# Longer TensorE matmul durations in the planner of an encoder block

## The chip, the cores and the metric

The kernel runs on one core of a Trainium2 chip. The metric is the device time of one execution in microseconds (us). Five engines run side by side, each with its own instruction stream taken in order: PE (TensorE, matmuls), DVE (VectorE), ACT (ScalarE), POOL (GpSimd) and SP (SyncE, which here issues DMAs).

## The reference

One layer of a hybrid encoder, 256 tokens with 16 meta tokens put in front (272 positions), width 2048, all in fp32:

```python
h = concat([meta, x])                               # 272 x 2048
hn = rmsnorm(h, mix_norm_g)
q_a, k_a, v_a, cq, ckv, k_pe = split(hn @ w_in)     # 3 x 1024, 512, 256, 64 columns
oa = neighbourhood_attention(q_a, k_a, v_a, ...)    # 8 heads of 128, window on a 4 x 64 grid
ob = mla_attention(cq, ckv, k_pe, ...)              # 8 heads; low-rank q and kv, rotary key
h = h + concat([rmsnorm(oa), rmsnorm(ob)]) @ w_out
hn = rmsnorm(h, ffn_norm_g)
g, u = hn @ w_gate, hn @ w_up                       # 2048 -> 5632
h = h + (silu(depthwise_conv3(g)) * u) @ w_down     # 5632 -> 2048
return h[:, 16:]                                    # meta tokens dropped
```

## The kernel before

**Arithmetic.** Every fp32 number is kept as two parts of a shorter fp32 format that PE takes faster (`F32R`): a high part, copied by ACT (`whi<-raw`, L251), and a low part, a subtract on DVE (`wlo<-raw,whi`, L255). A product of two such numbers is three matmuls: high by high, high by low, low by high. `mm3` (L734 to L736) issues these three for one 128 x 128 block of weights and 256 to 272 columns of tokens; `mm2` (L2056, L2057), in the MLP, puts the high and low part of the tokens beside each other in one matmul of 512 columns, with a second of 256. Other products go through `MM`, a list of matmuls whose lines are L291. Some of the MLP's weights go through a seven-product scheme (Strassen's, in Winograd's form), for which DVE adds and subtracts quarters of weight blocks (`more_raw`, `sums`) and of results (`mt`).

**Stages.** The program goes through the input projection with the two attentions woven into it (to about 300 us of the span), the output projection (to about 400 us), gate and up of the MLP (to about 850 us) and the down projection. Weights are read once, in pieces of 128 x 1024, in an order that is written out: `raw` (5 buffers) is filled by a DMA, split into `whi` and `wlo` (4 buffers each), and used by PE. The attention helpers are small chains between the large matmuls. The ones that the text speaks of:

- Sums over the head's dimension of squares (`late<-scr,late` on DVE, then the matmul pair `bank<-late,ones_r` on PE, in `keys`).
- Sums for the few meta queries (`small_sums`): a cast on DVE (`sq8r<-sq`, L267), a subtract on POOL (`sq8r<-sq,sq8r`, L279), then two-column matmuls (`bank<-ones_r,sq8r`, L291).
- The rotary embedding (`rope`): a DMA swaps the halves of a tile (`scr<-scr`), DVE multiplies with the tables (`scr<-scr,consts`), then follow `mqr`, the parts of the rotated queries. There are four pairs of heads on each side, so each chain comes four times or eight.

**What sets the order.** The kernel orders its instructions itself, when the program is built. Each piece of work is a Python generator, a thread, that yields requests: an engine with a duration in ns, a free buffer, or an event. `Flow.run` holds one clock for each engine and takes, again and again, the thread whose next step could start first: the larger of the engine's clock and the thread's own time with a latency (700 ns where PE follows another engine), then by priority, then by age. It sets the clock to start plus duration, and the thread then emits its instruction. So the order on each engine's stream follows from these clocks. The durations are formulas: 93 + 0.833 n for an ACT operation of n elements, 68 + 1.04 n on DVE, 90 + 2.7 n on POOL (3.9 n after 400 us), a DMA's bytes over 350 with 2000 ns more (3200 after 400 us). On the chip each engine takes its stream in order and waits by semaphores for what it needs, so a duration in the planner changes no instruction, only the order.

Of the kernel before, what the change touches and what calls it, by code (L numbers as in the profile page):

```python
# [17 lines left out]
SEQ = 256  # L18
# [200 lines left out]
def encoder_block(ctx: ExitStack, tc: tile.TileContext, io):  # L219
# [15 lines left out]
    def size(ap):  # L235
        n = 1
        for s in ap.shape[1:]:
            n *= s
        return n
# [37 lines left out]
    def PTT(out, a, b, op):  # L277
        yield "pool", 90 + (2.7 if fl.cur.t < 4e5 else 3.9) * size(out)
        nc.gpsimd.tensor_tensor(out, a, b, op)  # L279

    def cost(l, r):
        n, m = size(r), l.shape[-1]
        if r.dtype != F32R:
            return max(1.69 * n, 3.33 * m, 50)
        return 0.445 * n + 3 if n >= 256 else max(0.84 * n, 0.84 * m, 27)

    def MM(items):

        yield "pe", sum(cost(l, r) for _, l, r, _, _ in items)
        for o, l, r, start, stop in items:  # L290
            nc.tensor.matmul(o, l, r, start=start, stop=stop)  # L291
# [86 lines left out]
    class RowPair:  # L378
# [50 lines left out]
        def used(self, kind):  # L429
            self.left[kind] -= 1  # L430
            if self.left[kind] == 0:
                by_sums = kind in ("more", "sums") or kind == "two" and self.mode == "third"
                fl.put(made if by_sums else raws, self.at[kind])
# [102 lines left out]
    n = len(others) - BEHIND  # L536
# [174 lines left out]
    def block():  # L711

        p, o = pieces[at[0]], at[1]
        if o % p.step == 0:
            yield p.ready[o // p.step]
        return p.hi[:, o : o + P], p.lo[:, o : o + P]
# [13 lines left out]

    def mm3(ps, xhi, xlo, start, stop):
        whi, wlo = yield from block()
        yield "pe", 3 * (0.445 * size(xhi) + 3)
        nc.tensor.matmul(ps, whi, xhi, start=start, stop=False)  # L734
        nc.tensor.matmul(ps, whi, xlo, start=False, stop=False)  # L735
        nc.tensor.matmul(ps, wlo, xhi, start=False, stop=stop)  # L736
        used()
# [37 lines left out]
    for g in range(0, FC // 2 if MID_SUMS else 0, MID_SUMS or 1):  # L775
        n = min(MID_SUMS, FC // 2 - g)
# [971 lines left out]
    def project(tiles, n, slots=acc):  # L1748

        pss = []  # L1750
        for _ in range(tiles):
            pss.append((yield from one(slots)))
        for k in range(KC):
            if at[0] < 2:
                yield from first_products(pss, k, n)
                continue
            yield ev_xs[k]
            for ps in pss:
                yield from mm3(ps[:, :n], hl[k][:, 0, :n], hl[k][:, 1, :n], k == 0, k == KC - 1)
        return pss  # L1760
# [37 lines left out]
    def attention_weights():  # L1798
# [8 lines left out]
        def up_queries(m):  # L1807
            pss = []
            for c in range(3):
                ps = yield from one(acc)  # L1810
                for k in range(4):
                    yield ev_cq[k]
                    yield from mm3(ps[:, :NT], cq[k][0], cq[k][1], k == 0, k == 3)
                pss.append(ps)
            fl.spawn(mla_queries(m, pss))

        def up_keys(m):
            yield ev_ckv
            for c in range(2):
                ps = yield from one(acc)  # L1820
                for k in range(2):
                    yield from mm3(ps[:, :L], ckv[k][0], ckv[k][1], k == 0, k == 1)
                fl.spawn(mla_keys(m, c, ps))
# [228 lines left out]
    def mm2(ps, x, n, start, stop):  # L2052

        whi, wlo = yield from block()
        yield "pe", 347
        nc.tensor.matmul(ps, whi, x, start=start, stop=False)  # L2056
        nc.tensor.matmul(ps[:, :n], wlo, x[:, 0, :], start=False, stop=stop)  # L2057
        used()

    def mm_up(ps, k):  # L2060
        yield from mm2(ps, hl[k][:, :, :SEQ], SEQ, k == 0, k == KC - 1)

    def mlp_weights():
        pss, f = [], 0
        for p, kind, which, q in work:
            if kind in ("gate", "up"):
                if q == 0:
                    pss = []
                    for _ in range(2):
                        pss.append((yield from one(acc)))  # L2070
                for k in range(4 * q, 4 * q + 4):
                    for c in range(2):
                        yield from (mm_gate if kind == "gate" else mm_up)(pss[c], k)
                if q == 3:
                    for c in range(2):
                        fl.spawn((gated if kind == "gate" else tile_up)(2 * which + c, pss[c]))
                if kind == "up" and which == FC // 2 - 1:
                    hl_free(q)
            elif kind == "scheme":
                yield from scheme_products(p, which)  # L2080
            else:
                if f == 0:
                    ps = yield from one(acc)
                for _ in range(p.n // P):
                    yield ev_act[f]
                    if which < KC - ST - 1:
                        yield from mm2(ps, act[:, f], SEQ, f == 0, f == FC - 1)
                    else:
                        yield from mm3(
                            ps[:, :SEQ], act[:, f, 0, :], act[:, f, 1, :], f == 0, f == FC - 1  # L2090
                        )
                    f += 1
                if f == FC:
                    fl.spawn(down_out(which, ps))
                    f = 0
# [376 lines left out]
```

## Time and profile before

| | |
|---|---|
| time, median of 3 runs | 1103.25 us (1103.39, 1103.25, 1102.38) |
| span of the profiled execution | 1102.0 us; no time of its own is given beside it, the runs lie 0.4 to 1.4 us over it |
| granted clock of PE | 0.999 |
| busy: PE, DVE, ACT, POOL | 99%, 92%, 68%, 11% |
| instructions on PE, DVE, ACT, POOL | 8164, 1935, 1507, 199 |
| DMA, mean over the span | 238 GB/s |

The span is from the profiled execution's first instruction to its last. "Busy" is the share of the span in which an engine had an instruction under way. Matmuls overlap in PE's pipeline, so a row's duration (some 280 ns for 256 columns) is longer than the time from one start to the next; what a matmul costs in a full queue is that second time.

### The profile page before, as it was taken

The page shows a single profiled execution, that of the slowest core. Times are in us where ns is not written, and L with a number is a line of the kernel's source. Part 1 is how long each engine was busy: PE and PEld are TensorE (multiplying, and loading weights), DVE is VectorE, ACT ScalarE, POOL GpSimd, SP SyncE. Part 2 cuts the span into 40 slices and gives each one's busy share as a digit, 9 for nine tenths or more (in the row PEclk, how much of TensorE's full clock was granted, in tenths as well). Part 3 has the DMA queues.
Part 4 walks back from the last instruction along what each step waited for, and adds up shares of the span by engine and source line. Part 5 has one row for each costly group of instructions (what it writes and reads, how often), then busy time and mean ns, then how long its engine had stood idle before and what let it go on. Part 6 is the DMA issues. An engine that isn't in the chain of part 4 may idle for free.

```text
span 1102.0 us, 22408 instructions
## 1 busy us (share of the span) xinstructions
PE 1094.0 (99%) x8164; PEld 1046.5 (95%) x8164; DVE 1015.0 (92%) x1935; ACT 751.1 (68%) x1507; POOL 120.8 (11%) x199
## 2 busy tenths in 40 slices
PE   9999999999999999999999999999999999999998
PEld 9999999999999999999999999999999999888887
DVE  8969887988878989999999999999999989999997
ACT  8688978888646776656666666665666656566663
POOL 3211222232443400000000000000000000000001
PEclk9999999999999999999999999999999999999999
DMA  9765678567877778655666656758788878699891
GB/s 327 253 230 176 197 218 236 149 203 182 255 207 208 229 256 324 215 193 192 224 221 209 225 192 237 262 193 285 264 299 287 292 237 322 205 320 336 302 331 45
DMA packets 82166, 262.72 MB, mean 238 GB/s; under 512 B 9224, under 2 KB 13320, under 8 KB 82056
## 3 DMA queue, kind: packets, MB, share of 16 engines
q1 hardware_dynamic: 78600, 252.38, 66.0%
q0 software_dynamic: 3168, 8.65, 5.2%
q8 instruction: 64, 1.05, 0.4%
q14 instruction: 46, 0.38, 0.1%
q10 hardware_dynamic: 288, 0.27, 0.1%
HBM read 243.82 MB, written 34.08 MB: 252 GB/s over the span
## 4 chain that ended last, share of the span: by engine, by line
PE 87%; ACT 5%; DVE 4%; DMA 2%; issue 1%; SPq 0%; POOL 0%; DVEq 0%; ACTq 0%; POOLq 0%
PE bank L291 27%; PE bank L734 14%; PE bank L735 14%; PE bank L736 14%; PE bank L2056 11%; PE bank L2057 6%; PE bank L297 2%; ACT whi L251 1%; DVE wlo L255 1%; DVE scr L263 1%; ACT scr L251 1%; DMA scr<-scr 1%; ACT qraw L251 0%; DMA early<-in_w_down_s 0%; DMA raw<-in_w_cq 0%
## 5 line engine op out<-in xcount | busy, mean ns | idle before, releaser
L251 ACT ACTIVATE whi<-raw 128x512 fp32r<-128x512 f32 (+2 forms) x493 | 354.1, 738 | 158.5 <-PE bank L735 54.6
L255 DVE TENSOR_TENSOR wlo<-raw,whi 128x512 fp32r<-128x512 f32 (+2 forms) x493 | 408.0, 848 | 30.7 <-ACT whi L251 29.8
L734 PE MATMUL bank<-hl,whi 128*128 128x258 f32 (+1 forms) x1208 | 347.8, 288 | 0.1
L735 PE MATMUL bank<-hl,whi 128*128 128x258 f32 (+1 forms) x1208 | 343.7, 285 | 0.0
L736 PE MATMUL bank<-hl,wlo 128*128 128x258 f32 (+1 forms) x1208 | 343.1, 284 | 0.2 <-DVE wlo L255 0.2
L736 PEld LDWEIGHTS bank<-hl,wlo 128*128 128x128 f32 x1208 | 229.7, 190 | 0.6 <-DVE wlo L255 0.4
L735 PEld LDWEIGHTS bank<-hl,whi 128*128 128x128 f32 x1208 | 229.3, 190 | 0.1
L734 PEld LDWEIGHTS bank<-hl,whi 128*128 128x128 f32 x1208 | 228.2, 189 | 0.8 <-ACT scr L251 0.3
L291 PE MATMUL bank<-whi,act 128*128 128x256 f32 (+1 forms) x574 | 143.5, 302 | 0.0
L2056 PE MATMUL bank<-hl,whi 128*128 128x512 f32 x384 | 136.6, 395 | 0.0
L2057 PE MATMUL bank<-hl,wlo 128*128 128x256 f32 x384 | 107.7, 280 | 0.0
L291 PEld LDWEIGHTS bank<-whi,act 128*128 128x128 f32 x574 | 100.2, 189 | 5.2
L251 ACT ACTIVATE whi<-more_raw 128x1024 fp32r<-128x1024 f32 x69 | 71.8, 1040 | 42.7 <-DVE more_raw L255 22.7
L291 PE MATMUL bank<-wlo,act 128*128 128x256 f32 (+1 forms) x287 | 86.8, 302 | 0.0
L2056 PEld LDWEIGHTS bank<-hl,whi 128*128 128x128 f32 x384 | 72.1, 188 | 14.9
L255 DVE TENSOR_TENSOR wlo<-more_raw,whi 128x1024 fp32r<-128x1024 f32 x69 | 82.6, 1196 | 3.2 <-ACT whi L251 3.1
L279 POOL TENSOR_TENSOR halves<-halves,resT 128x256 f32<-128x256 f32 x4 | 3.0, 784 | 703.9 <-ACT halves L251 703.9
L2057 PEld LDWEIGHTS bank<-hl,wlo 128*128 128x128 f32 x384 | 72.4, 188 | 0.0
L291 PE MATMUL bank<-whi,sin 128*128 128x256 f32 (+1 forms) x248 | 69.0, 325 | 0.0
L251 ACT ACTIVATE whi<-halves 128x1024 fp32r<-128x1024 f32 (+2 forms) x57 | 52.2, 936 | 22.4 <-PE bank L291 7.5
L255 DVE TENSOR_TENSOR wlo<-halves,whi 128x1024 fp32r<-128x1024 f32 (+2 forms) x57 | 60.4, 1074 | 0.5 <-ACT whi L251 0.3
L291 PEld LDWEIGHTS bank<-wlo,act 128*128 128x128 f32 x287 | 54.3, 189 | 2.2
(323 smaller groups left out, 2216.1 us busy)
## 6 DMA issues: line engine op xcount, KB each, us to landing
raw<-in_w_gate SPq DMA_DIRECT2D x88, 512.0 KB, 5.1
raw<-in_w_in SPq DMA_DIRECT2D x52, 512.0 KB, 4.5
raw<-in_w_up SPq DMA_DIRECT2D x48, 512.0 KB, 4.5
raw<-in_w_up_s SPq DMA_DIRECT2D x40, 512.0 KB, 4.4
raw<-in_w_out SPq DMA_DIRECT2D x32, 512.0 KB, 5.1
sin<-s_down SPq DMA_DIRECT2D x28, 512.0 KB, 6.5
raw<-in_w_down_m SPq DMA_DIRECT2D x21, 512.0 KB, 5.4
s_down<-sums SPq DMA_DIRECT2D x20, 512.0 KB, 6.5
```

The lines of the kernel that those rows point to most:

```text
L251: nc.scalar.activation(out, in_, f, **kw)
L255: nc.vector.tensor_tensor(out, a, b, op)
L263: nc.vector.scalar_tensor_tensor(out, a, s, b, op0, op1)
L279: nc.gpsimd.tensor_tensor(out, a, b, op)
L291: nc.tensor.matmul(o, l, r, start=start, stop=stop)
L297: nc.tensor.transpose(o, i, ident[:n, :n])
L734: nc.tensor.matmul(ps, whi, xhi, start=start, stop=False)
L735: nc.tensor.matmul(ps, whi, xlo, start=False, stop=False)
L736: nc.tensor.matmul(ps, wlo, xhi, start=False, stop=stop)
L2056: nc.tensor.matmul(ps, whi, x, start=start, stop=False)
L2057: nc.tensor.matmul(ps[:, :n], wlo, x[:, 0, :], start=False, stop=stop)
```

## The change

The planner's duration of a large matmul is another formula; all else in the program text is the same.

```diff
+    def stream(n):
+        return n / 2.4 + 0.436 * -(-n // 16) + 4.7
+
     def cost(l, r):
         n, m = size(r), l.shape[-1]
         if r.dtype != F32R:
             return max(1.69 * n, 3.33 * m, 50)
-        return 0.445 * n + 3 if n >= 256 else max(0.84 * n, 0.84 * m, 27)
+        return stream(n) if n >= 256 else max(0.84 * n, 0.84 * m, 27)
...
     def mm3(ps, xhi, xlo, start, stop):
         whi, wlo = yield from block()
-        yield "pe", 3 * (0.445 * size(xhi) + 3)
+        yield "pe", 3 * stream(size(xhi))
...
     def mm2(ps, x, n, start, stop):
         whi, wlo = yield from block()
-        yield "pe", 347
+        yield "pe", stream(2 * SEQ) + stream(SEQ)
```

The formulas give, in ns: 118.3 for 116.9 at 256 columns, 119.6 for 117.8 at 258, 125.4 for 124.0 at 272, 232.0 for 230.8 at 512; a step of `mm2` 350.4 for 347.

The program has the same instructions on each engine. PE's are the same to the operand, except for the buffer in which a split weight or a helper's tile lies. On PE the first difference in order stands at row 254 (about 36 us), the last at row 3234 (about 400 us): between them the large matmuls keep their order, and the helpers' matmuls stand 3 to 40 matmuls earlier or later among them. On DVE some 1020 rows stand elsewhere, on ACT 700, on SP 236, on POOL 77, and these run to the end of the program. The new function moves the line numbers of all that follows by three.

In the order below a row is one instruction, or several alike (x2): line, operation, output and inputs (the number after a name is that of the tile or buffer), and the size. DVE, around 180 us, before; `late_164<-scr_176` is the last operand of the sum of squares for which PE waits at 185.55 us:

```order
L255 TENSOR_TENSOR wlo_92<-raw_84,whi_88 128x512
L267 CAST sq8r_212<-sq_210 128x8
L255 TENSOR_TENSOR scr_182<-scr_182,consts 128x258
L255 TENSOR_TENSOR wlo_89<-raw_80,whi_85 128x512
L263 SCALAR_TENSOR_TENSOR scr_177<-scr_183,scr_177 128x272
L263 SCALAR_TENSOR_TENSOR v_235<-cols_222,emc_c 128x4
L255 TENSOR_TENSOR wlo_89<-raw_80,whi_85 128x512
L263 SCALAR_TENSOR_TENSOR v_235<-bank_76,emc_s 4x1
L263 SCALAR_TENSOR_TENSOR scr_184<-scr_177,scr_184 128x272
L255 TENSOR_TENSOR mqr_265<-scr_178,mqr_265 64x258
L263 SCALAR_TENSOR_TENSOR scr_181<-scr_181,gains,scr_184 128x272
L255 TENSOR_TENSOR late_164<-scr_176,late_164 128x272
```

and with the change:

```order
L263 SCALAR_TENSOR_TENSOR scr_179<-scr_184,scr_179 128x272
L255 TENSOR_TENSOR wlo_92<-raw_84,whi_88 128x512
L263 SCALAR_TENSOR_TENSOR scr_182<-scr_179,scr_182 128x272
L255 TENSOR_TENSOR scr_177<-scr_177,consts 128x258
L267 CAST sq8r_212<-sq_210 128x8
L263 SCALAR_TENSOR_TENSOR scr_180<-scr_180,gains,scr_182 128x272
L255 TENSOR_TENSOR wlo_92<-raw_84,whi_88 128x512
L255 TENSOR_TENSOR wlo_89<-raw_80,whi_85 128x512
L255 TENSOR_TENSOR late_163<-scr_180,late_163 128x272
L255 TENSOR_TENSOR late_164<-scr_176,late_164 128x272
```

The rope product (`consts`) has gone from row 361 to row 355 of DVE and stands ahead of the `sq8r` cast instead of behind it; `late_164` has gone from row 370 to 361. The cast's own place has gone from row 360 to 356.

PE around 194.8 us, before, where the sums of the meta queries (`ones_r,sq8r_213`) follow an early block of weights:

```order
L735 MATMUL bank_72<-hl_100,whi_85 128x272
L736 MATMUL bank_72<-hl_100,wlo_89 128x272
L291 MATMUL bank_76<-ones_r,sq8r_213 4x2 x2
L734 MATMUL bank_75<-hl_100,whi_85 128x272
L735 MATMUL bank_75<-hl_100,whi_85 128x272
```

and with the change:

```order
L294 MATMUL bank_76<-mkp_268,qs_209 36x272
L737 MATMUL bank_75<-hl_101,whi_86 128x272
L738 MATMUL bank_75<-hl_101,whi_86 128x272
L739 MATMUL bank_75<-hl_101,wlo_90 128x272
L294 MATMUL bank_77<-ones_r,sq8r_213 4x2 x2
L737 MATMUL bank_72<-hl_101,whi_86 128x272
```

The sums now stand behind the next block of weights (`hl_101`) and behind the products with the small queries (`qs`), 37 matmuls later; the cast that feeds them stands at row 394 of DVE where it stood at 393.

DVE at 738 to 744 us, in the seven-product scheme, before:

```order
L255 TENSOR_TENSOR mt_5445<-mt_5445 128x128 x2
L255 TENSOR_TENSOR wlo_89<-more_raw_5449,whi_85 128x1024
L255 TENSOR_TENSOR sums_93<-mt_5445,sums_93 128x256
L255 TENSOR_TENSOR more_raw_5449<-raw_80 128x512
L255 TENSOR_TENSOR more_raw_5449<-raw_80,more_raw_5449 128x256
L255 TENSOR_TENSOR more_raw_5449<-more_raw_5449,raw_80 128x256
L255 TENSOR_TENSOR wlo_90<-raw_81,whi_86 128x1024
L255 TENSOR_TENSOR wlo_91<-raw_80,whi_87 128x512
L255 TENSOR_TENSOR wlo_91<-raw_80,whi_87 128x256
L255 TENSOR_TENSOR sums_93<-mt_5445,sums_93 128x256
```

and with the change:

```order
L255 TENSOR_TENSOR sums_93<-mt_5467,sums_93 128x256
L255 TENSOR_TENSOR wlo_89<-more_raw_5472,whi_85 128x1024
L255 TENSOR_TENSOR sums_93<-mt_5468,sums_93 128x256
L255 TENSOR_TENSOR more_raw_5472<-raw_84 128x512
L255 TENSOR_TENSOR more_raw_5472<-raw_84,more_raw_5472 128x256
L255 TENSOR_TENSOR more_raw_5472<-more_raw_5472,raw_84 128x256
L255 TENSOR_TENSOR wlo_90<-raw_81,whi_86 128x1024
L255 TENSOR_TENSOR wlo_91<-raw_84,whi_87 128x512
```

The second of the two `sums`, which stood behind the `wlo` pieces, now stands ahead of them, and the two `mt` have gone further up.

## The prediction

> **What bounds the kernel now.** I read the page first: the busy shares and the chain that ended last.
>
> ```profile
> span 1102.0 us, 22408 instructions
> PE 1094.0 (99%) x8164; PEld 1046.5 (95%) x8164; DVE 1015.0 (92%) x1935; ACT 751.1 (68%) x1507; POOL 120.8 (11%) x199
> PE 87%; ACT 5%; DVE 4%; DMA 2%; issue 1%; SPq 0%; POOL 0%; DVEq 0%; ACTq 0%; POOLq 0%
> ```
>
> TensorE (PE) is busy 99% of the span and carries 87% of the chain. A change that only reorders instructions, with the same matmuls, can therefore gain only what PE idles now, and can lose whatever new waits it puts in front of PE. So the next view is the table of busy time by window, where PE's idle time is the length of a window less its busy time.
>
> ```profile
> 0.00:50.00 50.00, 48.45 (x369) 47.47 (x370) 42.63 (x88) 38.87 (x88) 16.06 (x38) 1.00 0.86 305
> 50.00:100.00 50.00, 49.47 (x397) 48.14 (x396) 41.54 (x105) 40.87 (x122) 7.17 (x16) 1.00 0.59 196
> 100.00:150.00 50.00, 49.75 (x417) 49.02 (x416) 43.94 (x125) 44.90 (x150) 11.91 (x27) 1.00 0.67 203
> 150.00:200.00 50.00, 48.45 (x402) 47.87 (x401) 42.17 (x114) 41.18 (x131) 14.94 (x27) 1.00 0.76 220
> 250.00:300.00 50.00, 49.83 (x414) 49.32 (x413) 44.39 (x118) 38.65 (x116) 18.38 (x28) 1.00 0.78 216
> 300.00:400.00 100.00, 100.00 (x816) 99.14 (x815) 84.62 (x151) 63.45 (x125) 35.15 (x35) 1.00 0.76 224
> 600.00:700.00 100.00, 100.00 (x780) 97.17 (x779) 98.44 (x181) 63.49 (x102) 0.00 (x0) 1.00 0.64 224
> sum 1102.00, PE 1093.97 PEld 1046.54 DVE 1015.04 ACT 751.14 POOL 120.81; mean PE 78.14 PEld 74.75 DVE 72.50 ACT 53.65 POOL 8.63
> ```
>
> (Columns: window, its length, then busy us and count of PE, PEld, DVE, ACT, POOL, then the granted clock, DMA share, GB/s.) PE idles 1.55 us in the first 50 us, 0.53, 0.25 and 1.55 in the next three windows, 0.17 in 250:300, none in 300:400 and none in the MLP. That is 4.05 us; the sum row's 8.03 us holds besides it the last 4 us, when the output leaves. The list of waits names the causes:
>
> ```profile
> PE bank L291 <- POOL sq8r L279: 1.1, 3, 0.7
> PE bank L866 <- DVE em L863: 1.1, 1, 1.1
> PE bank L291 <- DVE late L255: 0.9, 1, 0.9
> PE bank L291 <- ACT whi L251: 0.3, 1, 0.3
> PE bank L736 <- DVE wlo L255: 0.2, 1, 0.2
> PE bank L291 <- ACT p L251: 0.2, 1, 0.2
> ```
>
> The `em` wait of 1.1 us is the start of the program; it stays. What reordering can take is 4.05 - 1.1 = 2.95 us, in the attention stage. One number decides what the new durations mean, the start-to-start time of matmuls in a full queue, from the chain of waits (start, length, what):
>
> ```profile
> 450.66 1.42 PE bank L291 x12
> 950.16 8.32 PE bank L291 x36
> ```
>
> 12 matmuls of 256 columns take 1.42 us, 118 ns each; 36 of 512 take 8.32 us, 231 ns each.
>
> **The change part by part.** Formula in `cost`: `stream(256)` is 256/2.4 + 0.436*16 + 4.7 = 118.3 ns, where 0.445*256 + 3 gave 116.9; `stream(512)` is 232.0 for 230.8. So the new values lie within 1 ns of the rows, the old ones 0.2 to 1 ns under them: about 1% on PE. `mm3` and `mm2` hold the same formula (3 x 119.6 = 358.8 ns for 353.4 at 258 columns; 350.4 for 347). The matmuls, their count and their operands stay, so the direct cost is nothing. What it adds is slip: in 4.5 us between two helper matmuls the planned PE clock comes about 0.05 us later, and ties between threads fall the other way. That moves instructions from about 36 us on (PE row 254) until about 400 us; in the MLP PE's order is as before, and only DVE, ACT and the DMA queues are rearranged around it.
>
> The Trainium skill, "TensorE: Matmul & The Clock Gate", section Part 1, has a warm matmul start N/2.4 GHz plus about 2.5 ns after the one before it: 215.7 ns at 512 columns. By that both formulas are too long and the change goes the wrong way, but the quoted chain has 231 ns, and the row decides; the sum is the same by either, since no duration on the chip is touched.
>
> *The two long waits.* PE's rows (start, us, engine line op, tiles, [idle before <- releaser]):
>
> ```profile
> 185.55 0.39 PE L291 MATMUL bank<-late,ones_r 128*128 128x272 f32 x1 [0.89 <-DVE late L255]
> 194.81 0.17 PE L291 MATMUL bank<-ones_r,sq8r 128*4 128x2 f32 x1 [0.67 <-POOL sq8r L279]
> 254.38 0.19 PE L291 MATMUL bank<-ones_r,sq8r 128*4 128x2 f32 x2 [0.17 <-ACT p L251]
> ```
>
> and DVE's timeline ahead of the first:
>
> ```profile
> 178.24 0.68 DVE L255 TENSOR_TENSOR wlo<-raw,whi 128x512 fp32r<-128x512 f32 x1
> 178.83 0.16 DVE L267 CAST sq8r<-sq 128x8 fp32r<-128x8 f32 x1
> 181.38 0.43 DVE L255 TENSOR_TENSOR scr<-scr,consts 128x258 f32<-128x258 f32 x1 [2.39 <-DMA scr<-scr]
> 181.72 0.69 DVE L255 TENSOR_TENSOR wlo<-raw,whi 128x512 fp32r<-128x512 f32 x1
> 182.33 0.98 DVE L263 SCALAR_TENSOR_TENSOR scr<-scr,scr 128x272 f32<-128x272 f32 x1
> 183.30 0.68 DVE L255 TENSOR_TENSOR wlo<-raw,whi 128x512 fp32r<-128x512 f32 x1
> 183.97 0.42 DVE L263 SCALAR_TENSOR_TENSOR scr<-scr,scr 128x272 f32<-128x272 f32 x1
> 184.32 0.41 DVE L255 TENSOR_TENSOR mqr<-scr,mqr 64x258 fp32r<-64x258 f32 x1
> 184.66 0.48 DVE L263 SCALAR_TENSOR_TENSOR scr<-scr,gains,scr 128x272 f32<-128x272 f32 x1
> 185.07 0.42 DVE L255 TENSOR_TENSOR late<-scr,late 128x272 fp32r<-128x272 f32 x1
> ```
>
> DVE works in order. It reaches the rope product `scr<-scr,consts` and stands 2.39 us until rope's swapped halves have landed; everything behind it is late, `late` among it, by which PE loses 0.89 us. From the start of the product to the end of `late` are 185.49 - 181.38 = 4.1 us. In the new DVE order the product stands six rows earlier, and the work from it to the same `late` is two `wlo` of 0.61, `sq8r` 0.16, three or four operations of 0.35 to 0.48: about 3.1 us at most, for the `late` that PE wants first. PE gets to its own row at the same distance behind. With 1.0 us less ahead of it, the 0.89 us go. But the cast of `sq8r`, which stood ahead of the rope product, now stands behind it. It needs the same DMA, then a subtract on POOL, before its small matmuls; before, it was 2.5 us earlier than the product. PE wants it 9 rows later than before, some 9 x 0.12 = 1.1 us. I bound this new wait by 0 (enough cover) and by 2.39 us less those 1.1, 1.3 us; I take 0.5, nearer the low end since the wait at the DMA ends at least part of its way into the cover.
>
> The wait at 194.81: PE's row for the second `sq8r` goes 37 matmuls back in PE's order, 37 x 0.12 = 4.4 us of cover, while DVE's cast moves by one row (under 0.7 us): the 0.67 us go. At 254.38 PE's row moves back by 8 places, 1 us, over a wait of 0.17: that goes. Gone together: 0.89 + 0.67 + 0.17 = 1.73 us.
>
> *What comes in their place.* The remaining 2.95 - 1.73 = 1.2 us of short waits sit at the other seams of the attention stage, where everything moves too. What made all of these waits is untouched: the scheduler holds a 1024-column subtract at 68 + 1.04*1024 = 1133 ns and a DMA at its bytes over 350 plus 2 us, and the trace has
>
> ```profile
> L255 DVE TENSOR_TENSOR wlo<-raw,whi 128x1024 fp32r<-128x1024 f32 x161 | 196.1, 1220 | 15.5 <-ACT whi L251 15.1
> DMA to landing us min/median/max: 1.8/5.8/9.0
> ```
>
> (the second row is of the tile `scr`, which rope's swaps fill, between 60 and 300 us). A planner with those errors makes a fresh draw of misplacements at each new order. I price the draw by what this one cost: 1.73 us for the part that moved, of which 0.5 is the `sq8r` above and 1.2 are places I can't name. Its bounds are 0 and twice as much, 3.5 us.
>
> *The MLP.* PE never waits, but DVE is busy 98.44 of 100 us in 600:700, so its order matters. The tightest place is this (two rows of DVE, one of PE):
>
> ```profile
> 739.75 0.42 DVE L255 TENSOR_TENSOR sums<-mt,sums 128x256 fp32r<-128x256 f32 x1
> 741.61 2.16 DVE L255 TENSOR_TENSOR wlo<-raw,whi 128x1024 fp32r<-128x1024 f32 x3
> 743.17 0.28 PE L736 MATMUL bank<-hl,wlo 128*128 128x258 f32 x1
> ```
>
> The first of the three `wlo` (1.22 us) ends at 742.83, 0.34 us before PE reads it. In the new order one more `sums` of 128x256 (0.42 us here) stands ahead of it: 0.34 - 0.42 = -0.08. The same pattern stands at 543, 609 and 676 us with some 0.46 us of slack. So 0.1 us is lost, between 0 and 0.5 us (all four by a whole 0.1 us or so). The rows from there to the end keep their order on PE and their slack.
>
> *Sum*, against the profiled execution's own 1102.0 us, which is 1.25 under the median of 1103.25: -1.73 + 0.5 + 1.2 + 0.1 = +0.1 us, so 1103.3 on the median's scale. I call a change of 0.2%, 2.2 us, the least that can be told from none.
>
> **The rivals.**
>
> *Faster: the waits go and nothing comes.* For it: the two longest waits are removed by causes that I can follow row by row, and the new PE durations are nearer to the chip's. Against: the other errors of the plan are larger (1220 for 1133 ns is 8%, PE's was 1%). Without the unnamed 1.2: -1.73 + 0.5 + 0.1 = -1.1 us, 1102.1, still within 0.2%. To pass 2.2 us, `sq8r` must cost nothing and at least 0.5 of the other 1.2 us vanish too: 1103.25 - 2.4 = 1100.8. Only the latter counts as faster.
>
> *Slower: rope's DMA holds DVE where PE has no cover.* One mechanism: in the new order a rope product again stands ahead of something that PE wants soon, as at 181.38, but with a late landing. In before, DVE lost 2.39 us there and PE 0.89. A landing of 9.0 us, the longest of the row above, comes 3.2 us after the median of 5.8; PE then loses 0.89 + 3.2 = 4.1 us at one place, in place of the 0.5 taken. That gives 1103.3 + 3.6 = 1106.9. It decides from a landing of about 8 us at one of the four pairs of heads. For it: the product stands earlier in the new order, so it is likelier reached before its data. Against: the median landing, and POOL and ACT feed it first.
>
> *Slower: DVE in the MLP.* If the rearranged `sums` and `more_raw` rows cost PE 0.1 us at each of some twenty blocks instead of four, it is 2 us: 1105.3. The point from which it decides is slack under 0.42 us, and only one place of the trace is below that.
>
> *The clock.* Every window above but the last is granted 1.00. If a wait of the new order let the granted clock fall to a half, each matmul of 256 columns after it would take 236 ns for 118, and 2 us of such work cost 2 us more: 1105.3. The Trainium skill, "TensorE: Matmul & The Clock Gate", section Part 1, has the clock halved after an idle window of about 3.4 us; by that only the late-landing rival above could come near it, and the sum and every other case stand as they are. The longest wait in the list is 1.1 us and left the clock at 1.00, so I give this 0.01, inside slower.
>
> *The change does nothing.* If DVE's and ACT's waits absorbed the moves, the time would be the median, 1103.25. It can't be told from my forecast by time, only by the waits.
>
> **How the numbers follow.** No change within 0.2% (the sum, the small faster case and the change that does nothing): 0.65. Faster by over 0.2%: 0.15. Slower: 0.20, of which 0.12 is the late landing, 0.07 DVE in the MLP, 0.01 the clock. Time 1103.3. The range: down to 1100.7, where all 1.73 and most of the 1.2 us are gone; up to 1106.3, which holds the 3.5 us bound of new waits with 0.5 of `sq8r` in it, the MLP bound 0.5 and the 0.89 + 0.67 of the gain that stay unspent only in part, and leaves the worst late landing out. About 0.1 lies on either side.
>
> **What would show it.** In the waits of after: no `late` wait near 185 us and no `sq8r` wait near 195, in their place `sq8r` near 184 to 186 behind a DMA `scr<-scr`; a sum of PE's waits between 2 and 5 us; PE's busy column 100.00 in every window from 300 to 900. If it shows the same 0.9 and 0.7 us at the same operations, my reading of the order is wrong. If PE's busy column drops by over 0.5 us in an MLP window, the DVE term was mis-sized; if one wait is over 2 us, the late landing came.

## The result, and the profile after

The changed kernel takes 1114.55 us (median of 4, 1113.02 to 1115.03) where the kernel before, run beside it, takes 1103.32 (1102.38 to 1104.12): 1.0098 of the time, 95% interval 1.0085 to 1.0111. It is 11 us slower; the forecast was no change, with 1106.3 as the upper end. The span went from 1102.0 to 1112.1 us. The page's busy times and its chain, after:

```profile
span 1112.1 us, 22402 instructions
PE 1098.9 (99%) x8164; PEld 1047.4 (94%) x8164; DVE 1019.2 (92%) x1935; ACT 749.0 (67%) x1507; POOL 119.6 (11%) x199
PE 72%; DVE 16%; ACT 5%; issue 4%; DMA 2%; POOL 1%; SPq 0%; DVEq 0%; ACTq 0%; POOLq 0%
```

The shares of busy time hardly moved. The chain of work that ended last shows the change: PE's share of it fell from 87% to 72%, DVE's rose from 4% to 16%. The windows tell where (length, then PE, PEld, DVE, ACT, POOL, clock, DMA, GB/s):

```profile
50.00:100.00 50.00, 48.46 (x389) 47.01 (x388) 40.89 (x106) 40.58 (x121) 8.33 (x16) 1.00 0.56 186
100.00:150.00 50.00, 48.40 (x400) 47.11 (x400) 41.28 (x116) 42.33 (x141) 12.20 (x27) 1.00 0.71 218
150.00:200.00 50.00, 48.83 (x402) 47.94 (x401) 44.79 (x113) 42.04 (x133) 14.87 (x27) 1.00 0.73 210
200.00:250.00 50.00, 49.40 (x410) 48.49 (x409) 42.10 (x111) 42.25 (x129) 13.48 (x23) 1.00 0.64 174
400.00:500.00 100.00, 98.18 (x742) 94.08 (x740) 89.36 (x165) 64.05 (x104) 0.00 (x0) 1.00 0.72 242
500.00:600.00 100.00, 99.73 (x800) 97.94 (x799) 98.30 (x187) 63.90 (x104) 0.00 (x0) 1.00 0.62 204
600.00:700.00 100.00, 99.45 (x776) 96.50 (x775) 98.13 (x176) 62.38 (x98) 0.00 (x0) 1.00 0.67 224
800.00:1100.00 300.00, 300.00 (x1836) 268.01 (x1836) 286.78 (x417) 188.10 (x253) 0.00 (x0) 1.00 0.81 278
```

PE idles 1.54, 1.60, 1.17 and 0.60 us in the four attention windows from 50 to 250 us, 1.82 us at the MLP's start, and 0.27 to 0.55 us in each later 100 us up to 800. From 800 on it has no idle time, and the clock is at 1.00 throughout. Idle time understates the loss, since a matmul's end overlaps the next one's start. A fuller measure is the sum, over PE's rows in the trace, of start-to-start time less that of a bare matmul (the change's formula for large ones, 109 ns for a transpose, 213 ns for each of the 14 rows of fp32 matmuls at the start, 27 ns for a small one). Called **PE's excess** below, it was 12.2 us before and is 22.3 after: 10.1 us more, the whole growth of the span between the two traces. To 400 us it went from 10.6 to 15.9, behind 400 us from 1.5 to 6.4. The medians lie 11.2 us apart; the other 1.1 is the trace of before, whose span of 1102.0 us is 1.2 over the median of that kernel's other executions (1100.8). PE's waits, and four of the rows:

```profile
PE bank L739 <- DVE wlo L255: 2.9, 6, 1.3
PE bank L300 <- POOL p L279: 1.9, 4, 0.9
PE bank L294 <- POOL sq8r L279: 1.8, 5, 0.8
PE bank L294 <- DVE v L263: 0.7, 1, 0.7
```

```profile
75.56 0.22 PE L294 MATMUL bank<-ones_r,sq8r 128*4 128x2 f32 x3 [0.82 <-POOL sq8r L279]
136.32 0.33 PE L300 MATMUL bank<-ident,p 128*128 128x128 f32 x1 [0.86 <-POOL p L279]
445.31 0.39 PE L739 MATMUL bank<-hl,wlo 128*128 128x258 f32 x1 [1.32 <-DVE wlo L255]
752.89 0.39 PE L739 MATMUL bank<-hl,wlo 128*128 128x258 f32 x1 [0.27 <-DVE wlo L255]
```

(0.27 us of idle time at 752.89 are 0.43 of excess, start to start. The same wait stands at 551, 618 and 685 us.) There are two losses then: many waits for helpers in attention, and waits for the low part of weights, `wlo`, in the MLP. Attention shows 26 gaps over 150 ns to 400 us, for 15 before.

### The profile page after: what moved, and what is told of

It reads as the page before. It is cut to its first block, busy times and chain, and to the rows that moved or that the text cites. A ratio compares the mean times of both kernels' runs of the same rounds, so it can differ in the third digit from the quotient of the medians.

```text
span 1112.1 us, 22402 instructions
## 1 busy us (share of the span) xinstructions
PE 1098.9 (99%) x8164; PEld 1047.4 (94%) x8164; DVE 1019.2 (92%) x1935; ACT 749.0 (67%) x1507; POOL 119.6 (11%) x199
## 4 chain that ended last, share of the span: by engine, by line
PE 72%; DVE 16%; ACT 5%; issue 4%; DMA 2%; POOL 1%; SPq 0%; DVEq 0%; ACTq 0%; POOLq 0%
PE bank L294 21%; PE bank L739 11%; PE bank L737 11%; PE bank L738 11%; PE bank L2059 10%; DVE wlo L255 8%; PE bank L2060 5%; ACT whi L251 2%; DVE more_raw L255 2%; PE bank L300 2%; DVE mt L255 1%; ACT scr L251 1%; DVE scr L263 1%; DMA raw<-in_w_cq 1%; DVE mt L263 1%
```

## The experiments

Each is compared with the kernel before on the same chip. "To 400" and "from 400" are PE's excess in the profiled run; the kernel before has 10.6 and 1.5.

### Which stage

`attention_only` uses the new durations while the planner's clock is under 400 us, `mlp_only` after it:

```diff
     def stream(n):
+        if fl.cur.t >= 4e5:              # mlp_only: < 4e5
+            return 0.445 * n + 3
         return n / 2.4 + 0.436 * -(-n // 16) + 4.7
```

(and 347 for `mm2` under the same condition).

> The new durations only while the planner's clock is under 400 us (attention and output projection, order on PE and DVE there as in the changed kernel); the old ones after. Theory 1, two losses: the change loses about 5.3 us in the attention stage (short waits of PE on sums and transposes) and about 4.9 us in the MLP, each by its own stage's order; then this run loses 5 us: 1107.5 to 1109.5. Theory 2, handed on: the MLP is late because attention left DVE late; then all of it is lost here: 1112 to 1115. Rival 3, only the MLP counts: 1103 to 1104.5.

> The old durations while the planner's clock is under 400 us (order there as before), the new ones after. Theory 1: only the MLP's share is lost, 1107 to 1109, with PE waits for wlo at about 440, 460 and once in each block of 67 us. Theory 2 (the loss comes out of attention): 1103 to 1104.5. Rival 3: 1112 to 1115.

`attention_only`: 1111.24 us, ratio 1.0071 [1.0056, 1.0086]; to 400: 16.5, from 400: 3.2. `mlp_only`: 1105.03, 1.0016 [1.0006, 1.0026]; to 400: 8.5, from 400: 4.0. Both times lie between the ranges of theory 1 and theory 2 and in neither. There are two losses, as theory 1 has it, but not of its sizes: attention alone loses 7.9 us and the MLP alone 1.6, and 1.7 more come when both are together (11.2 less 9.5). As theory 2 has it, part of what is lost in the MLP is handed on by attention: `attention_only` has 3.2 us from 400 us on for the 1.5 of before. `mlp_only` keeps the order before until the MLP and has the four waits of 0.43 us at 541, 608, 675 and 743. The wait at the MLP's start needs the new attention order: 0.77 us at 445 in `attention_only`, none in `mlp_only`, 1.48 and 0.67 with both.

`mlp_only` also shows something of the kernel before. With the same order to 400 us, its list of PE's waits has no `late`, and rope's product waits for its DMA

```profile
179.39 0.43 DVE L255 TENSOR_TENSOR scr<-scr,consts 128x258 f32<-128x258 f32 x1 [0.53 <-DMA scr<-scr]
```

0.53 us for the 2.39 of the profile of before. In the four other kernels below with that attention order it waits 0.81 to 1.36 us, and PE never waits for `late` there. So the 0.89 us belonged to one execution, not to the order. The wait of 0.67 us for `sq8r` near 195 us came back in two of those five kernels, as 0.37 in a third.

### What the MLP's blocks are short of

In three blocks of the MLP, from one of the waits at 543 or 541 us to the fourth, the windows read, before and in `mlp_only`:

```profile
543.20:743.20 200.00, 200.00 (x1587) 195.76 (x1586) 196.87 (x364) 128.30 (x202) 0.00 (x0) 1.00 0.64 222
```

```profile
541.40:743.00 201.60, 200.76 (x1584) 195.93 (x1584) 197.94 (x365) 126.90 (x202) 0.00 (x0) 1.00 0.67 220
```

In neither does DVE wait for another engine: its list of waits there is empty, and its longest gap is 0.11 us. So in the kernel before both PE and DVE work without a pause through a block of 66.66 us, and any more of DVE's time must lengthen it. Its 363 operations are the same in `mlp_only`, but take 1.5 us more, start to start. The place is in the timeline of `mlp_only`:

```profile
538.67 0.68 DVE L255 TENSOR_TENSOR more_raw<-raw 128x512 f32<-128x512 f32 x1
539.39 0.42 DVE L255 TENSOR_TENSOR more_raw<-raw,more_raw 128x256 f32<-128x256 f32 x1
539.85 0.43 DVE L255 TENSOR_TENSOR more_raw<-more_raw,raw 128x256 f32<-128x256 f32 x1
540.20 1.82 DVE L255 TENSOR_TENSOR wlo<-raw,whi 128x1024 fp32r<-128x1024 f32 x2
```

The second and third rows are alike in size, 128x256. After the second 0.46 us pass to the next start, after the third 0.35. The third reads what the second has just written, while `wlo` does not read `more_raw`. Such a neighbour costs 118 ns (median of 213 pairs in the program before). An operation that overwrites what the one ahead of it read costs as much (120 ns, median of 44). In the three blocks `mlp_only` has 12 more of the two kinds, six of each: six after an `mt<-mt` (three of either kind), three that read after `mt<-mt,vecs,mt`, and three after `wlo<-more_raw`, where `more_raw` is filled anew. 12 x 0.118 = 1.4 of the 1.5 us. The planner's 68 + 1.04 n has no such term. To test whether DVE's total or the place of a single subtract makes the waits:

```diff
 # before_more_dve, in finish_value
         yield from TT(act[:, f, 1, :], u_, act[:, f, 0, :].bitcast(F32), ALU.subtract)
+        nc.vector.tensor_tensor(act[:, f, 1, :], u_, act[:, f, 0, :].bitcast(F32), ALU.subtract)
 # mlp_only_less_dve, for odd f instead of that TT
+            yield "dve", 68 + 1.04 * SEQ
+            nc.gpsimd.tensor_tensor(act[:, f, 1, :], u_, act[:, f, 0, :].bitcast(F32), ALU.subtract)
```

> The kernel before, with the subtract that makes the low part of each tile of the MLP's activations (128x256, 0.33 us of DVE, 44 in the program) issued twice in a row; the planner isn't told, so the order is the one before. Theory edge (DVE's work for a block of 67 us is within 0.2 us of PE's, so any more of it becomes PE waits): six more such operations per block are 2.0 us, the blocks lose about 1.8 us each, 8 to 14 us in all: 1111 to 1117. Theory order (PE waits in the blocks because a subtract stands behind something, not for DVE's total): under 3 us, 1103 to 1106.

> The kernel with the new durations in the MLP alone, and every second of these low-part subtracts on POOL, which idles there; the planner still counts them on DVE, so the rest of the order stays. DVE has 1.0 us less in each block. Theory edge: the four waits of 0.43 us are gone, 1102.5 to 1104. Theory order: the waits stay, as what stands ahead of the late subtract is the same, 1104.5 to 1106. If POOL and DVE hinder each other, DVE's rows grow and it is over 1106.

`before_more_dve`: 1114.59 us, 1.0104 [1.0087, 1.0121]; from 400: 13.2. 11.4 us of excess came in 500 to 800 us, where 26 of the 44 doubled subtracts stand. Each costs DVE 0.46 us and not the 0.33 of the expectation: the pair takes 0.452 + 0.343 us start to start, a single one 0.335, so the second, which rewrites what the first wrote, also starts 117 ns later. 26 x 0.46 = 12.0 us, and PE lost 11.4 of them. The edge is shown: DVE has next to no slack there. `mlp_only_less_dve` went the other way, as the third of its expectations has it (over 1106 if POOL and DVE hinder each other): 1106.74, 1.0034 [1.0021, 1.0047]; the waits grew to 0.53 to 0.81 us. The rows of 500 to 800 us tell why (first the moved operation on POOL and those that stayed on DVE, then `wlo` of 128x512):

```profile
L1971 POOL TENSOR_TENSOR act<-mt,act 128x256 fp32r<-128x256 f32 x13 | 12.6, 971 | 288.6 <-ACT act L251 225.5 <-DMA sin<-s_down 61.1 <-DMA raw<-in_w_up_s 2.1
L255 DVE TENSOR_TENSOR act<-mt,act 128x256 fp32r<-128x256 f32 x13 | 6.7, 517 | 0.0
L255 DVE TENSOR_TENSOR wlo<-raw,whi 128x512 fp32r<-128x512 f32 x35 | 25.3, 722 | 0.0
```

and of `mlp_only`, the same two on DVE:

```profile
L255 DVE TENSOR_TENSOR act<-mt,act 128x256 fp32r<-128x256 f32 x26 | 10.5, 418 | 0.0
L255 DVE TENSOR_TENSOR wlo<-raw,whi 128x512 fp32r<-128x512 f32 x36 | 24.6, 684 | 0.0
```

A POOL operation takes 0.64 us, every third one 1.1 (one of 3.5 lifts the mean to 0.97), and about one DVE operation grows beside each (12 for the 13 of POOL): a `wlo` of 128x1024 from 1.22 to 1.67 us, one of 128x512 from 0.68 to 1.13, `act` from 0.41 to 0.86. In three blocks nine operations less saved DVE 3.0 us, and those left took 4.35 us more. This run relieved DVE of nothing, so it decides nothing between the two theories; it is a point on how the two engines share.

### Spreading the neighbours

The rule: between 400 and 780 us of the planner's clock, a helper that has just used DVE may use it again only after 118 ns, so that another thread's operation goes between.

```diff
         if th.eng == eng and (eng == "pe" or callable(th.prio) or th.prio >= 2):
-            return 0.0
+            return 118.0 if eng == "dve" and 4e5 <= th.t < 7.8e5 else 0.0
```

> New durations in the MLP alone, and between 400 and 780 us of the planner's clock a thread of the MLP's helpers may take DVE again only 118 ns after its last DVE operation, so the planner puts another thread's work between a writer and its reader. Pairs of neighbours on DVE in which the second reads what the first wrote fall from 222 to 100 in the program. Theory pairs (each such pair costs DVE some 118 ns; the new MLP order has 12 more of them in three blocks, which makes a block 67.0 us of DVE where PE has 66.66): DVE's time for a block falls by 1.5 us or more, the four waits of 0.43 us go, 1102.5 to 1103.7. Theory place (a subtract stands behind something): the waits stay, 1104.5 to 1106.

> The same rule in the kernel before. Attention's order is the one before. Theory pairs: DVE's time for a block falls by over 1 us, but PE sets the pace there already, so the time stays: 1102.8 to 1103.8. A draw in the MLP too: 1104 to 1107.

> The same rule in the changed kernel, whose attention order stays. Theory pairs: the block waits go (2.1 us) and DVE has time to catch up at the MLP's start, where PE waits 2.1 us: 1110 to 1112.7, with the attention stage's loss as it is. If the MLP's start has another cause: 1112 to 1113. Theory place: 1113 to 1115.

`mlp_only_spread`: 1102.84, 0.9998 [0.9989, 1.0006]; from 400: 1.8. `before_spread`: 1102.35, 0.9995 [0.9986, 1.0004], so it isn't shown to be faster. `after_spread`: 1109.93, 1.0063 [1.0049, 1.0076]; to 400: 16.2, from 400: 1.8. The windows of `after_spread`:

```profile
400.00:500.00 100.00, 100.00 (x756) 96.11 (x755) 89.80 (x170) 65.89 (x108) 0.00 (x0) 1.00 0.72 248
600.00:700.00 100.00, 100.00 (x780) 97.18 (x779) 95.59 (x177) 63.10 (x99) 0.00 (x0) 1.00 0.69 224
```

PE is full again, at the MLP's start too. In `mlp_only_spread`, DVE's list of waits in three blocks, empty before, has now

```profile
DVE wlo L255 <- ACT whi L251: 4.9, 9, 0.9
```

so DVE gets ahead and waits for ACT. Theory pairs holds (`after_spread` and `before_spread` lie 0.1 and 0.5 us under its ranges). For the MLP's share of the change the rule is worth 4.5 us of excess from 400 us on (6.4 to 1.8), 3.5 parts in a thousand of the time. One lucky order of the MLP isn't behind it: in all seven kernels with the rule, these three and the four with a margin below, the excess from 400 us on is 1.5 to 1.8. What is left of the change's loss lies in attention.

### Attention: direction or draw

First, other durations with the formulas of before: all PE durations times a factor, or POOL's raised to what the trace shows.

```diff
-        return 0.445 * n + 3 if n >= 256 ...
+        return F * (0.445 * n + 3) if n >= 256 ...     # the same in mm3 and mm2; F = 0.99, 1.002, 1.012
 # pool_true
-        yield "pool", 90 + (2.7 if fl.cur.t < 4e5 else 3.9) * size(out)
+        yield "pool", 330 + 2.7 * size(out) if fl.cur.t < 4e5 else 90 + 3.9 * size(out)
-        yield "pool", 150        # three casts and copies
+        yield "pool", 330
```

> All matmul durations of the old formulas times 0.99, the other direction. Theory direction (longer PE durations put the low-part subtracts later in DVE's order): no loss in the MLP, 1100 to 1104 in all. Theory draw (the order before is a lucky one among many, in attention above all): the MLP as before, but attention loses as much as by the change, 1106 to 1110. If held PE durations matter only through truth: worse than the change, over 1114.

> All matmul durations of the old formulas times 1.002, a sixth of the change. Theory direction, in proportion: 1104.5 to 1106. Theory draw: attention loses 2 to 6 us at once, the MLP little, 1105 to 1110. No effect of so small a step: 1103 to 1104.

> All matmul durations of the old formulas times 1.012, the mean size of the change by another formula; in the planner's own clocks PE never idles between 100 and 400 us in it, as in the kernel before, where the changed kernel has 2.1 us of idle time. Theory size (1.2% more is what costs attention its time): attention as in the changed kernel, 1111 to 1115. Theory draw with the planner as judge (an order is good when PE doesn't idle in the plan): attention as before, and the MLP's 2 to 4 us: 1105 to 1108. Theory blind draw: anything between 1106 and 1113.

> The kernel before with POOL's durations in the planner raised to what the trace shows until 400 us: 330 + 2.7 n for 90 + 2.7 n, 330 for 150 in the casts (the trace has 367 ns for 128x16, 308 to 434 for the casts). Theory draw (any new order of the attention stage costs some us): 1105 to 1110, with other waits. Theory truth (waits for POOL's p and sq8r come from POOL held too short): 1101 to 1103.5.

> The changed kernel with the same POOL durations. Theory truth: the waits for POOL's p and sq8r, about 6 us of the attention stage's 9.7 in the changed kernel, shrink to under 2 us: 1108 to 1111. Theory draw: other waits of the same sum, 1112 to 1117.

All lose. `pe_099`: 1107.42, 1.0036 [1.0024, 1.0047]. `pe_1002`: 1105.92, 1.0023 [1.0014, 1.0032]. `pe_1012`: 1111.71, 1.0077 [1.0064, 1.0091]. `before_pool_true`: 1107.70, 1.0042 [1.0027, 1.0057]. `after_pool_true`: 1111.14, 1.0076 [1.0061, 1.0091]. Neither shorter nor longer PE durations, nor truer ones for POOL, give an order as good as the one before, and a step of a sixth of the change costs 2.5 us. The draw's ranges hold `pe_099`, `pe_1002` (whose time fits a loss in proportion as well) and `before_pool_true`. The time of `pe_1012` lies in the range of theory size, but by other shares than that theory has: 12.4 us to 400 for the change's 15.9, and 7.7 from 400. `after_pool_true` lies between its two ranges. Its excess is 15.4 to 400 and 4.0 from 400, so most of what it gains on the changed kernel is the MLP's. The waits change their names: in `after_pool_true` PE waits for none of POOL's results, but

```profile
PE bank L294 <- ACT p L251: 2.4, 4, 0.9
PE bank L294 <- DVE mkp L255: 1.1, 1, 1.1
```

so truer durations for POOL took its waits away and others came in their place: 15.4 us of excess for 15.9. Nor does the planner's own clock judge an order: in `pe_1012` its PE never idles between 100 and 400 us, and the chip's PE loses 12.4 us to 400.

Then I compared where the helpers' matmuls stand in PE's order, counted in weight matmuls ahead of them. The change puts them 5.4 earlier on average (534 matmuls), 0.64 us at 120 ns. Where the planner holds PE slower, the same chain on DVE, ACT and POOL seems to need fewer of PE's matmuls for cover; this is argued and no run shows it by itself. The last four runs move them by a margin for helpers, with the MLP's rule in all:

```diff
         if eng == "pe":
-            return self.TO_PE
+            return self.TO_PE + (M if th.prio == 0 and th.t < 4e5 else 0)     # M = 600, 300, -300, 300
```

> The changed kernel with the MLP's rule for neighbours on DVE (as in after_spread, 1109.9), and until 400 us the planner holds a matmul of an attention helper possible 600 ns later after another engine's result than before (1300 for 700 ns). In PE's order the helpers' matmuls then stand 6.9 weight matmuls later on average than in the kernel before, where the change put them 5.4 earlier. Theory cover (the change costs attention its time because helper matmuls went forward in PE's order by 0.64 us on average, so their operands are not ready): PE's loss in attention falls from 16 us over the bare matmuls to 8 to 11, 1102 to 1105. Theory draw (any order but the one before loses): 12 to 16 us, 1106 to 1110.

> The same with 300 ns; the helpers' matmuls stand 2.5 weight matmuls earlier than in the kernel before. Theory cover: between the two, 11 to 14 us lost in attention, 1105 to 1108. Theory draw: 11 to 16, no order with the other runs, 1105 to 1110.

> The kernel before with the MLP's rule (as in before_spread, 1102.35), and 300 ns less for attention helpers (400 for 700 ns): the helpers' matmuls stand 9.8 weight matmuls earlier, with the old durations of matmuls. Theory cover: attention loses as much as in the changed kernel or more, 15 to 20 us over the bare matmuls for 9, 1108 to 1114. Theory draw: 11 to 14, 1104 to 1108.

> The same with 300 ns more: helpers' matmuls 7.1 weight matmuls later. Theory cover: no more waits than before, 7 to 10 us over the bare matmuls, 1100.5 to 1103.5; a version at least as fast as the kernel before. Theory draw: 11 to 14 us, 1104 to 1108.

| kernel | helpers' matmuls, mean shift | PE's excess to 400 us | time, ratio |
|---|---|---|---|
| attention order of before (6 kernels) | 0 | 8.5, 8.9, 9.2, 9.4, 10.0, 10.6 | |
| pe_099 | -1.0 | 12.2 | 1.0036 |
| pe_1002 | -1.8 | 11.5 | 1.0023 |
| before_pool_true | -2.3 | 13.1 | 1.0042 |
| after_margin_300 | -2.5 | 13.3 | 1106.90, 1.0038 [1.0024, 1.0053] |
| before_margin_300 | +7.1 | 13.4 | 1106.93, 1.0039 [1.0025, 1.0053] |
| after_margin_600 | +6.9 | 13.1 | 1106.48, 1.0034 [1.0022, 1.0046] |
| after, attention_only, after_spread | -5.4 | 15.9, 16.5, 16.2 | 1.0098, 1.0071, 1.0063 |
| pe_1012 | -5.7 | 12.4 | 1.0077 |
| after_pool_true | -7.6 | 15.4 | 1.0076 |
| before_margin_m300 | -9.8 | 17.5 | 1109.58, 1.0064 [1.0049, 1.0079] |

Neither theory holds alone. Cover foretold 8 to 11 us for `after_margin_600` and 7 to 10 for `before_margin_300`; they lost 13. A draw foretold 11 to 14 for `before_margin_m300`; it lost 17.5. What fits: each of the ten other orders loses at least 2 to 4 us over the order before (mean 9.4), wherever its helpers stand on average, and three of the four that put them forward by 5 or more lose 3 to 5 on top, with old and with new durations. Executions of one order differ less: 8.5 to 10.6 for the order before, 15.9 to 16.5 for the change's. `pe_1012` is the exception and leaves this a tendency. Taken one by one, the helpers' matmuls say the same. Over the ten orders, of those that moved forward by three or more weight matmuls 81 of 2665 start over 0.15 us later than behind a bare matmul, of those that moved back as far 16 of 1889; in the order before it is 7 of 566. A new order moves some forward even where the mean goes back (136 with `after_margin_600`). That would be the price of any draw, but the operands' own chains move too, and no run separates the two. With the margin, the changed kernel gets back 3.4 us of `after_spread`'s loss (1109.93 to 1106.48). Why each single wait came is open, and so is why the order before has so few.

No kernel tried is shown to beat the one before; `before_spread` equals it.

## Why the prediction was wrong, point by point

The sum was -1.73 + 0.5 + 1.2 + 0.1 = +0.1 us. Between the two traces it is +10.1: 5.3 us of PE's excess in attention, where the sum has 0.0, and 4.8 from 400 us on, where it has 0.1. The path was right (no cost on PE itself, only waits). The steps that failed are a gain that wasn't there, the price of a new order in attention, and the MLP's slack.

- **The bound and the place.** Right: PE is the bound, the loss is new waits and nothing else, it begins in attention, the end of the program from 800 us on is as before, and the clock stays at 1.00. The Trainium skill's shorter start-to-start time ("TensorE: Matmul & The Clock Gate", section Part 1) played no part, as the prediction had it: the rows after the change still have 231 ns at 512 columns, where it gives 215.7.
- **"Gone together: 1.73 us."** The `sq8r` waits at 194.8 and 254.4 went, and the one at 185.6 gave way to an `sq8r` wait at 185.2 (0.30 us start to start, 0.5 forecast) and a `late` wait at 188.3 (0.83). But 0.89 of the 1.73 wasn't there to be gained: with the order before, five other profiled runs have no such wait. The step that failed took a wait behind a DMA in one execution for a property of the order. The scale shows the same: the prediction set this trace 1.25 us under the median, but it compared a span with times. Spans lie 2.0 to 2.5 us under the times, and 1102.0 is 1.2 over the median span of the other executions.
- **"What comes in their place": 0.5 + 1.2 us, bound 3.5.** This term was mis-sized. Taking the new waits as equal to those that go assumed that the order before was an ordinary one. Ten other orders of that stage are all worse by 2 us or more, so it was a rare one, and the fair price of leaving it was some 3 us. Another 3 to 5 us tend to come with helpers that go forward; the changed order has 5.3 more than the trace of before, 6.5 more than the mean of that order's six.
- **The planner's errors.** The argument "1220 for 1133 ns is 8%" was a misreading. A row's duration overlaps the next one: of a 1024-column subtract the next starts 1.14 us later, as the planner has it (1.139 us is the mean over the 48 of them in three blocks, before and after). The missing term was the 118 ns between neighbours.
- **"The MLP: 0.1 us, between 0 and 0.5."** Measured 4.8 us of excess: 2.2 in 400 to 500 us, 2.2 in 500 to 800, 0.3 later. The slack of 0.34 us at one `wlo` was read as a reserve of each place by itself. It was a lead that DVE, without a pause, could not win back, and DVE had some 1.5 us more to do in three blocks. By the prediction's own test (PE's busy column down by over 0.5 us in an MLP window: 1.82 and 0.55) this term was mis-sized. The rival "DVE in the MLP" named the mechanism's engine, at 0.07 and 2 us; its condition, a slack under 0.42 us at one place, wasn't what decided. The MLP's start, 1.5 + 0.7 us, was in no term.
- **The late landing** (0.12) didn't come: no wait is over 1.32 us.

## What to carry to other kernels

A list-scheduled order that runs PE at 99% is one point, and here all ten neighbours tried in one stage were worse: truer durations for one engine redraw the whole order, so price the draw (here 2 to 4 us of 1100, up to 8) ahead of any named gain, and bring it back with other constants or keep the order. Where two engines both run without a pause, slack at a place is no reserve; count the other engine's whole time, with the gaps between dependent neighbours. And look for a wait behind a DMA in a second execution before counting on its end.

## What the runs showed of the hardware

- On DVE an operation that reads what the one ahead of it wrote starts 118 ns later than an independent one (median of 213); one that overwrites what the one ahead read, 120 ns (median of 44); the doubled subtract, which rewrites what the one ahead wrote, 117 ns. Spreading the first two kinds took DVE's busy time, in 600 to 700 us, from 98.13 to 95.59 us of 100.
- POOL's work slows DVE's. A 128x256 subtract of 0.64 us or more on POOL cost DVE some 0.48 us on average (4.35 us over nine), more than the 0.33 us that it takes on DVE itself; a 128x1024 `wlo` beside it took 1.67 us for 1.22.
- Some waits repeat closely between executions of one order (the one at 75 us is 0.43 to 0.44 us in six, the four in the MLP 0.42 to 0.44 in two kernels). DVE's at rope's DMA does not (0.53 to 2.39 us), nor PE's for `sq8r` near 195 us (none to 0.67).
